# A hybrid token-mixer block: the scan's x tiles in two tiles of their own, requested two chunks ahead

## The chip, the cores and the metric

The kernel runs on one core of a Trainium2 chip. The metric is the device time of one execution in microseconds (us). Three executions of the kernel before took 1987.88, 1989.72 and 1990.76 us; their median, 1989.72 us, is the time that a change is held against. One further execution was profiled.

## What is computed

The reference is one layer of a streaming encoder over 1024 frames of width 1024, in float32. One input projection feeds three mixers that run side by side (latent attention, attention with forgetting, and a Mamba-2 scan), three sigmoid gates weigh them, and a gated feed-forward block with a short convolution follows. The change lies in the scan. Cut to it, the reference is:

```python
xBC = jax.nn.silu(causal_dwconv(xBC, conv_w, conv_b))
xs, Bm, Cm = jnp.split(xBC, [SSM_INNER, SSM_INNER + SSM_GROUPS * SSM_STATE], axis=-1)
...
xdt = xf * dtc[..., None]
cb = jnp.einsum('bcign,bcjgn->bcijg', Cc, Bc)
y_diag = jnp.einsum('bcijg,bcijgh,bcjghp->bcighp', cb, decay, xdt)
states = jnp.einsum('bcjgn,bcjgh,bcjghp->bcghpn', Bc, decay_to_end, xdt)
_, h_in = lax.scan(step, h0, (jnp.moveaxis(states, 1, 0), jnp.moveaxis(chunk_decay, 1, 0)))
y_off = jnp.einsum('bcign,bcghpn,bcigh->bcighp', Cc, h_in, jnp.exp(a_cum))
y = (y + xh * D[:, None]).reshape(Bsz, S, SSM_INNER)
return rms_norm(y * jax.nn.silu(z), norm_g)
```

The kernel scans in chunks of 128 frames, eight in all (`NT` = 8).

## The kernel before, in words

The work runs in stages, one behind the other on TensorE: projections, the convolution that makes x, B and C for the scan and stores them to `xbc_d` in DRAM (about 390 to 540 us of the profile), the two attentions (540 to 878 us), the scan (878 to about 1080 us), the branch projections, and the feed-forward block. Every matmul with two float32 operands is made of three products of high and low halves, so an operand is split first: ScalarE (ACT) writes the high half, VectorE (DVE) the low one.

The scan alone does not fill TensorE. So the attentions and the scan are interleaved with *fill*: the projections of the gates (`all_fill`, L1410 on, matmuls `mm` on L1428). A fill block loads a weight tile `wr` (L1392), splits it into `wh` and `wl` (L1399, L1400), makes two half-rows of a gate in PSUM, sends each through a tanh on ACT (L1406) into a row buffer `u`, and stores the row to `g_d` (L1438).

The row buffers are a ring of four tiles of 128x1024 float32 (`f_t4`, L1382, tag `t4`). Three kinds of tiles take turns in it: the fill's rows `u`, the scan's gate rows `zt` (L1968), and the scan's x tiles `xs` (L1906). All of them appear in the profile under the name `t`.

One chunk c of the scan goes through three steps.

- `ssd_a` (L1913): request B and C (`bc`) and the decay rows (`row`) of chunk c+1; transpose the eight 128x128 blocks of `xs` in two groups of four (`stp`, L1922), each copied by ACT into `xT` (L1923); request `xs` of chunk c+1 (L1927); transpose B and multiply C by B (L1933, L1935, into one `stp` tile), which DVE and ACT read on L1936 to L1938 (`bT` high and low, and `cbm`); then `xd` (DVE, L1941), `xdd` and `y` (GpSimd, L1945 and L1947), the split of `xdd` into `xddh` and `xddl`, and the decay matrices `E` (ACT L1954 and L1955, DVE L1956).
- `ssd_b` (L1966) one chunk later: request `zt`; the states (`pst`, L1964), the state `hst` (DVE L1979 to L1982), the products `py` (L1990), the part from the state before (`pof`) and the scaled output (L2008 to L2017, with a reciprocal root that goes back and forth between DVE and GpSimd).
- `ssd_c` (L2019) one more chunk later: transposes of the output (`stp`, L2025), copies to `yT` (L2026), and the store.

All `stp` tiles, whatever their step, take turns in two PSUM buffers (tag `tp`, two buffers): a transpose group waits until the readers of the group two before it are done.

What sets the order. TensorE runs in program order inside `manual_schedule`, and the program order comes from `merge` (L1470 on), which interleaves the three steps and the fill by a planned cost of each. The other engines and the DMA queue of the sync engine (SP) are ordered by the scheduler of the language, when the program is built; each then runs strictly in its order. Every load and store that matters here is issued on SP, so an issue that has to wait holds up all that stand behind it.

The pool `frp` (L1889) is opened ahead of the scan. In the kernel before its two tiles, `ws0` and `ws1` of 128x1024 float32, are first used after the scan, for two rows of attention output (`ar`, L2104) and then for sums of feed-forward weights (`ws_tiles`, L2069).

Of the kernel before, what the change touches and what calls it, by code (L numbers as in the profile page):

```python
# [11 lines left out]
F32 = mybir.dt.float32  # L12
# [9 lines left out]
P = 128  # L22
D = 1024
S = 1024
NT = S // P
# [17 lines left out]
def block_kernel(ctx: ExitStack, tc: tile.TileContext, x, positions, norm_mix_g, w_in, b_gate,  # L43
# [7 lines left out]
    def TP(name, bufs, **kw):  # L51
        if kw.get("space") != DRAM:
            kw["reuse_waits"] = "tile"
        return tc.tile_pool(name=name, bufs=bufs, **kw)
# [72 lines left out]
    def uid(s):  # L127
        cnt[0] += 1
        return f"{s}_{cnt[0]}"

    def split(h, l, src, he=None, le=None):
        he = he or A
        le = le or V
        i = A.activation(h, src, AF.Copy) if he is A else he.tensor_copy(h, src)  # L134
        return i, le.tensor_sub(l, src, f32(h))  # L135
# [489 lines left out]
    with ExitStack() as pm:  # L625
# [165 lines left out]
        def fx_bank():  # L791
            return acc("fx", "mv" if units % 3 == 2 else "mm")
# [243 lines left out]
    with ExitStack() as px:  # L1036
# [70 lines left out]
        for n, (which, c0) in enumerate(chunks):  # L1107
# [11 lines left out]
            for t in range(NT):  # L1119
# [8 lines left out]
                p = fx_head[t] if units < 6 else fx_bank()  # L1128
# [30 lines left out]
        for half in range(2):  # L1159
            p = fx_bank()  # L1160
# [30 lines left out]
    with ExitStack() as pc_:  # L1191
# [24 lines left out]
        def c_bank():  # L1216
            return psp.tile([P, 512], F32, name=uid("cb"), tag="up", bufs=6)
# [98 lines left out]
        for half in range(2):  # L1316
            p = c_bank()
# [64 lines left out]
    f_t4 = Ring(fpl, [P, S], F32, "t4", 4)  # L1382
# [67 lines left out]
    def advance(gen):  # L1450
        c = next(gen, None)
        while isinstance(c, list):
            for h in c:
                force(h)
            c = next(gen, None)
        if c is not None:
            clk[0] += c
            run_until(clk[0])
        return c
# [429 lines left out]
    frp = pfr.enter_context(TP("frp", 1, side="right"))  # L1889
    with ExitStack() as ps__:  # L1890
# [4 lines left out]
        def load_rows(o, c):  # L1895
            o.row = pool.tile([P, 16, P], F32, name=uid("row"), tag="row")
            for g in range(2):
                SY.dma_start(o.row[:, 8 * g:8 * g + 8, :],
                             cum_d[16 * c + 8 * g:16 * c + 8 * g + 8, :].partition_broadcast(P))

        def load_bc(o, c):
            o.bc = pool.tile([P, 4, P], F32, name=uid("bc"), tag="bc", bufs=3)
            SY.dma_start(o.bc, xbc_d[8:12, :, c * P:c * P + P].rearrange("j p s -> p j s"))

        def load_xs(o, c):
            o.xs, _ = f_t4.get()  # L1906
            o.xs = o.xs.rearrange("p (j s) -> p j s", j=8)
            SY.dma_start(o.xs, xbc_d[0:8, :, c * P:c * P + P].rearrange("j p s -> p j s"))

        def hb(t, c, hs=slice(0, 16)):  # L1910
            return t[:, c, hs].unsqueeze(2).to_broadcast([P, hs.stop - hs.start, 64])

        def ssd_a(o, c):  # L1913

            if c + 1 < NT:
                load_bc(obj[c + 1], c + 1)
                load_rows(obj[c + 1], c + 1)
            xT = pool.tile([P, D], F32, name=uid("xT"), tag="xT", bufs=1)
            for g in range(2):
                pt = psp.tile([P, 512], F32, name=uid("stp"), tag="tp", bufs=2)  # L1920
                for j in range(4):
                    T.transpose(pt[:, j * P:j * P + P], o.xs[:, 4 * g + j, :], ident)  # L1922
                A.activation(xT[:, 512 * g:512 * g + 512], pt, AF.Copy)  # L1923
                yield 0.44
            yield 0.0
            if c + 1 < NT:
                load_xs(obj[c + 1], c + 1)  # L1927
            o.bT = [pool.tile([P, 2, P], F32R, name=uid(n), tag=n) for n in ("bTh", "bTl")]
            o.c_ = [pool.tile([P, 2, P], F32R, name=uid(n), tag=n) for n in ("Ch", "Cl")]
            cbm = pool.tile([P, 2, P], F32, name=uid("cbm"), tag="cbm")  # L1930
            pt = psp.tile([P, 4, P], F32, name=uid("stp"), tag="tp", bufs=2)
            for g in range(2):
                T.transpose(pt[:, g, :], o.bc[:, g, :], ident)  # L1933
            for g in range(2):
                T.matmul(pt[:, 2 + g, :], o.bc[:, g, :], o.bc[:, 2 + g, :], start=True, stop=True)  # L1935
            split(*o.bT, pt[:, 0:2, :])  # L1936
            split(*o.c_, o.bc[:, 2:4, :])
            V.tensor_mul(cbm, pt[:, 2:4, :], tri.unsqueeze(1).to_broadcast([P, 2, P]))  # L1938
            xv = xT.rearrange("p (h d) -> p h d", d=64)
            o.xd = pool.tile([P, 16, 64], F32, name=uid("xd"), tag="xd")  # L1940
            V.tensor_mul(o.xd, xv, hb(dt, c))  # L1941
            o.xdd = [pool.tile([P, 16, 64], F32R, name=uid(n), tag=n, bufs=1) for n in ("xddh", "xddl")]
            xdd = pool.tile([P, 16, 64], F32, name=uid("xdd"), tag="xdd", bufs=1)
            if c + 1 < NT:
                G.tensor_mul(xdd, xv, hb(dend, c))  # L1945
            o.y = pool.tile([P, 16, 64], F32, name=uid("y"), tag="y", bufs=3)
            G.tensor_mul(o.y, xv, Db.unsqueeze(2).to_broadcast([P, 16, 64]))  # L1947
            yield 0.65
            o.E = []
            for q in range(4):  # L1950
                E = pool.tile([P, 4, P], F32, name=uid("E"), tag="E", bufs=4)
                for hh in range(4):
                    h = 4 * q + hh
                    A.activation(E[:, hh, :], o.row[:, h, :], AF.Relu, scale=-1.0, bias=cumc[:, c, h:h + 1])  # L1954
                A.activation(E, E, AF.Exp, scale=-1.0)  # L1955
                V.tensor_mul(E, E, cbm[:, q // 2:q // 2 + 1, :].to_broadcast([P, 4, P]))  # L1956
                o.E.append(E)
                if q == 1 and c + 1 < NT:
                    split(*o.xdd, xdd)
                yield 0.0  # L1960
# [71 lines left out]
        with tc.manual_schedule(engines={mybir.EngineType.PE}):  # L2032
            obj = {c: Head() for c in range(NT)}
            load_bc(obj[0], 0)
            load_xs(obj[0], 0)
            load_rows(obj[0], 0)
            merge([], 6.0)
            grain[0] = 4
            for c in range(NT + 2):
                st = []  # L2040
                if c < NT:
                    st.append((ssd_a(obj[c], c), 1.6))
                if 0 <= c - 2 < NT:
                    st.append((ssd_c(obj[c - 2], c - 2), *((0.88, 0.6) if c <= NT else (8.0, 0.2))))
                if 0 <= c - 1 < NT:
                    st.append((ssd_b(obj[c - 1], c - 1, obj.get(c - 2)), 6.4, 0.05))
                merge(st, FILL_SSD[c])
            for _ in range(4):
                if advance(fill) is None:
                    break  # L2050
# [234 lines left out]
    for t, nh in units:  # L2285
# [20 lines left out]
        p = head[t] if early else psp.tile([P, 512], F32, name=uid("wo"), tag="up", bufs=6)  # L2306
# [323 lines left out]
```

## Time and profile before

| | |
|---|---|
| median of three executions (lowest to highest) | 1989.72 us (1987.88 to 1990.76) |
| profiled execution, its own time | 1986.64 us |
| its span, first to last instruction | 1984.9 us |
| TensorE (PE) busy | 1958.7 us, 99% of the span |
| VectorE (DVE) / ScalarE (ACT) / GpSimd (POOL) busy | 70% / 49% / 35% |
| mean granted TensorE clock | 0.998 of full speed |

How to read the profile: all times are in us from the start of the span. A row of the timeline gives start, length, engine, line, operation, `output<-inputs` and, in brackets, how long the engine stood idle before the row and what ended that. `SPq` rows are issues of DMAs, not the transfers. A row of the chain of waits gives start and length of a piece of the chain that ended last. Matmuls overlap, so on PE the spacing of starts tells more than the length of one.

### The profile page before, as it was taken

What the parts mean: (1) busy time and instruction counts of PE and PEld (TensorE: products, weight loads), DVE (VectorE), ACT (ScalarE), POOL (GpSimd) and SP (SyncE); (2) the same over time, 40 slices, a digit from 0 to 9 for tenths busy, and PEclk for the clock granted to TensorE, in tenths of its full rate; (3) what the DMA queues carried; (4) which work ended last, traced back from release to release, by engine and by line L of the source; (5) the groups of instructions that cost most, each with busy time, mean ns of one, the idle gap of its engine ahead of it and who ended that gap; (6) DMA issues with size and microseconds to landing.
All of it is one profiled execution on the core that took longest, in us unless ns stands there. A gap on an engine that the chain in (4) does not pass through costs nothing.

```text
span 1984.9 us, 28475 instructions
## 1 busy us (share of the span) xinstructions
PE 1958.7 (99%) x10101; PEld 1668.1 (84%) x10101; DVE 1397.4 (70%) x2156; ACT 965.8 (49%) x1678; POOL 701.3 (35%) x666
## 2 busy tenths in 40 slices
PE   9999999999999999998999999999999999999999
PEld 8989888888899988887888888888878888888887
DVE  7777567879566766757884575558997777766555
ACT  5555322355466666766774232225554444544432
POOL 5133232056123222213340351101664444423655
PEclk9999999999999999999999999999999999999999
DMA  6166856333645556545665785333323211249575
GB/s 180 53 197 212 269 189 211 103 106 112 197 123 145 134 144 149 145 127 172 179 193 172 260 289 190 124 121 107 106 85 96 75 53 54 85 157 333 194 260 191
DMA packets 278409, 312.18 MB, mean 157 GB/s; under 512 B 19213, under 2 KB 209305, under 8 KB 278266
## 3 DMA queue, kind: packets, MB, share of 16 engines
q1 hardware_dynamic: 278264, 310.35, 50.5%
q8 instruction: 80, 1.31, 0.3%
q14 instruction: 63, 0.52, 0.1%
q10 hardware_dynamic: 2, 0.00, 0.0%
HBM read 217.17 MB, written 93.13 MB: 156 GB/s over the span
## 4 chain that ended last, share of the span: by engine, by line
PE 88%; DVE 4%; issue 3%; DMA 2%; ACT 2%; POOL 1%; SPq 0%; DVEq 0%; ACTq 0%; POOLq 0%
PE mm L1428 10%; PE dn L2577 10%; PE ybr L2145 9%; PE fx L798 7%; PE cb L1224 7%; PE ua L2236 6%; PE uc L2236 5%; PE ud L2236 5%; PE wo L2281 4%; PE s L1737 4%; PE tp L1804 3%; PE ub L2236 2%; PE fxv L188 2%; PE py L1990 1%; PE o L1824 1%
## 5 line engine op out<-in xcount | busy, mean ns | idle before, releaser
L1764 POOL TENSOR_SCALAR pm<-pm,rs 128x128 f32<-128x128 f32 (+7 forms) x128 | 95.2, 748 | 249.7 <-DVE rs L1762 217.3
L2577 PE MATMUL dn<-dr,dr 128*128 128x512 f32 x592 | 182.3, 389 | 0.0
L1428 PE MATMUL mm<-hnh,wh 128*128 128x512 f32 x320 | 133.1, 416 | 0.9 <-DVE o L1788 0.9
L2577 PEld LDWEIGHTS dn<-dr,dr 128*128 128x128 f32 x592 | 111.1, 188 | 22.9
L1428 PE MATMUL mm<-hnh,wl 128*128 128x512 f32 x320 | 126.4, 395 | 0.0
L1428 PE MATMUL mm<-hnl,wh 128*128 128x512 f32 x320 | 126.3, 395 | 0.0
L1756 ACT ACTIVATE pm<-s,nmx 128x128 f32<-128x128 f32 (+7 forms) x128 | 94.8, 741 | 64.6 <-DVE nmx L1751 56.3
L2577 PE MATMUL dn<-dr 128*128 128x512 f32 x296 | 115.3, 390 | 0.0
L1812 DVE TENSOR_TENSOR ptl<-tp,pth 128x512 fp32r<-128x512 f32 (+1 forms) x160 | 96.7, 631 | 24.5 <-ACT pth L1808 22.6
L135 DVE TENSOR_TENSOR dr<-dr,dr 128x1024 fp32r<-128x1024 f32 x52 | 73.0, 1413 | 51.2 <-ACT dr L134 41.8
L135 DVE TENSOR_TENSOR wl<-S,wh 128x1024 fp32r<-128x1024 f32 x55 | 82.9, 1507 | 34.8 <-ACT wh L134 34.8
L1751 DVE TENSOR_REDUCE nmx<-s 128x1 f32<-128x128 f32 (+7 forms) x128 | 93.5, 747 | 11.9 <-PE s L1737 7.4
L2145 PE MATMUL ybr<-al,wh 128*128 128x512 f32 x256 | 99.8, 390 | 0.0
L2145 PE MATMUL ybr<-ah,wl 128*128 128x512 f32 x256 | 99.8, 390 | 0.0
L2145 PE MATMUL ybr<-ah,wh 128*128 128x512 f32 x256 | 99.7, 389 | 0.0
L1808 ACT ACTIVATE pth<-tp 128x512 fp32r<-128x512 f32 (+1 forms) x160 | 82.6, 552 | 20.6 <-PE tp L1804 18.7
L134 ACT ACTIVATE wh<-wr 128x1024 fp32r<-128x1024 f32 (+1 forms) x47 | 42.4, 902 | 100.5 <-PE ybr L2145 39.5
L134 ACT ACTIVATE wh<-S 128x1024 fp32r<-128x1024 f32 x55 | 58.3, 1059 | 65.1 <-PE uc L2236 47.1
L134 ACT ACTIVATE dr<-dr 128x1024 fp32r<-128x1024 f32 x52 | 55.0, 1061 | 71.5 <-PE dn L2577 49.8
L1804 PE MATMUL tp<-ident,pm 128*128 128x128 f32 x576 | 81.1, 272 | 0.0
L135 DVE TENSOR_TENSOR wl<-wr,wh 128x1024 fp32r<-128x1024 f32 (+1 forms) x47 | 55.1, 1172 | 36.3 <-ACT wh L134 36.2
L2454 DVE SCALAR_TENSOR_TENSOR fa<-cg,pc_f,fa 128x1023 f32<-128x1023 f32 (+1 forms) x44 | 74.3, 1688 | 1.4 <-ACT fa L2449 1.4
(612 smaller groups left out, 6220.2 us busy)
## 6 DMA issues: line engine op xcount, KB each, us to landing
dr<-act_d SPq DMA_DIRECT2D x99, 256.0 KB
wr<-in_w_in_dram SPq DMA_DIRECT2D x35, 512.0 KB
gl<-g_d SPq DMA_DIRECT2D x24, 512.0 KB
wr<-in_ffn_w_up_dram SPq DMA_DIRECT2D x23, 512.0 KB
ws<-in_ffn_w_down_dram SPq DMA_DIRECT2D x22, 512.0 KB
wsum_d<-ws SPq DMA_DIRECT2D x22, 512.0 KB
act_d<-fa SPq DMA_DIRECT2D x22, 512.0 KB
g_d<-t SPq DMA_DIRECT2D x20, 512.0 KB
```

Source lines behind the costliest of these rows:

```text
L134: i = A.activation(h, src, AF.Copy) if he is A else he.tensor_copy(h, src)
L135: return i, le.tensor_sub(l, src, f32(h))
L798: T.matmul(p, a(k), b(k), start=k == 0 and i == 0, stop=k == NK - 1 and i == 2)
L1224: T.matmul(ps, a, b, start=first and i == 0, stop=i == 11, skip_group_check=not first)
L1428: T.matmul(ps, a[:, k, :], b[half][:, k, :], start=(k == 0 and i == 0), stop=(k == NK - 1 and i == 2))
L1756: A.activation(r.p[:, 0:cols], r.row, AF.Exp, bias=r.nmx[:, 0:1], accum_out=r.rs[:, 0:1])
L1764: r.norm = Task("G", (d - 0.025, d), lambda: G.tensor_scalar(r.p[:, 0:cols], r.p[:, 0:cols], r.rs[:, 1:2], 0.0, op0=ALU.mult, op1=ALU.add) ...
L1804: T.transpose(x.pt[:, c * P:c * P + P], rows_[qi].p[:, k * P:k * P + P], ident)
L1812: V.tensor_sub(x.tl[:, :off], x.pt[:, :off], f32(x.th[:, :off]))
L2145: T.matmul(pss[half], w_[:, k, :], a_[k][:, hs], start=k == 0 and i == 0, stop=k == nk - 1 and i == 2)
L2236: T.matmul(ps, a, b, start=first and n == 0, stop=n == 11, skip_group_check=not first)
L2577: T.matmul(ps[m], a[:, ts_], b[:, 512:], start=first_ and j == 0 and q == 0, stop=j == NFH - 1 and q == 2, skip_group_check=not first_)
```

## The change

The x tile of a chunk is no longer taken from the ring `f_t4`. It gets one of the two tiles `ws0` and `ws1` of the pool `frp`, the even chunks the first and the odd ones the second. The tiles of chunks 0 and 1 are requested ahead of the scan's loop, and chunk c requests the tile of c+2, instead of c+1, once its own transposes are in the program. The ring's four buffers are left to `u` and `zt`. Two tiles that live in `frp` after the scan (`ar`, L2104) now wait for the transposes of the last two x tiles.

```diff
         def load_xs(o, c):
-            o.xs, _ = f_t4.get()
-            o.xs = o.xs.rearrange("p (j s) -> p j s", j=8)
+            o.xs = frp.tile([P, 2, 512], F32, name=uid("xs"), tag=f"ws{c % 2}").rearrange(
+                "p a s -> p (a s)").rearrange("p (j s) -> p j s", j=8)
             SY.dma_start(o.xs, xbc_d[0:8, :, c * P:c * P + P].rearrange("j p s -> p j s"))
...
             yield 0.0
-            if c + 1 < NT:
-                load_xs(obj[c + 1], c + 1)
+            if c + 2 < NT:
+                load_xs(obj[c + 2], c + 2)
...
             load_bc(obj[0], 0)
-            load_xs(obj[0], 0)
+            for c in range(2):
+                load_xs(obj[c], c)
             load_rows(obj[0], 0)
```

The order of TensorE's and GpSimd's instructions is unchanged; only the name of the x tile differs in it. SP's queue changes at many places, DVE's and ACT's order at one place each (on ACT, the exponential of one `E` tile of chunk 2 and one tanh of the fill change places).

The first place is SP's queue at the end of the convolution stage and the beginning of the attentions. `xbc_d<-ca` is the last store of the convolution's output, `wr` a fill weight, `g_d` the gates' rows, `vv` and `qk` the values and the query and key tiles of the first attention heads. Before:

```order
L1238 DMA xbc_d<-ca_5757 128x1024
L1392 DMA wr_6379<-in_w_in_dram 128x8x128
L1309 DMA g_d_83<-cg_5692 128x1024
L1527 DMA vv_5892<-v_d 128x8x128
L1309 DMA g_d_83<-cv_5802 128x1024
L1522 DMA qk_1090_5894<-k_h 104x1024
```

In the same place now:

```order
L1238 DMA xbc_d<-ca_5757 128x1024
L1908 DMA xs_10582<-xbc_d 128x8x128
L1908 DMA xs_10584<-xbc_d 128x8x128
L1392 DMA wr_6379<-in_w_in_dram 128x8x128
L1309 DMA g_d_83<-cg_5692 128x1024
L1309 DMA g_d_83<-cv_5802 128x1024
L1527 DMA vv_5892<-v_d 128x8x128
L1522 DMA qk_1090_5894<-k_h 104x1024
```

The loads of the x tiles of chunks 0 and 1 stand right behind that store, ahead of both attentions, and the values of head 0 (`vv_5892`) stand behind one store more than before.

The second place is SP's queue at the beginning of the scan. `t<-xbc_d` is an x tile in the ring (the first row here is that of chunk 1, the second that of chunk 2), `t<-z_d` the `zt` of chunk 0, `g_d<-t` a fill row. Before:

```order
L1903 DMA bc_10753<-xbc_d 128x4x128
L1392 DMA wr_10821<-in_w_in_dram 128x8x128
L1898 DMA row_10755<-cum_d 128x1024 x2
L1438 DMA g_d_82<-t_2336_10591 128x1024
L1908 DMA t_2355_10697<-xbc_d 128x8x128
L1969 DMA t_2376_10778<-z_d 128x1024
L1908 DMA t_2394_10854<-xbc_d 128x8x128
L1903 DMA bc_10946<-xbc_d 128x4x128
```

In the same place now:

```order
L1903 DMA bc_10755<-xbc_d 128x4x128
L1392 DMA wr_10823<-in_w_in_dram 128x8x128
L1908 DMA xs_10699<-xbc_d 128x8x128
L1898 DMA row_10757<-cum_d 128x1024 x2
L1438 DMA g_d_82<-t_2337_10593 128x1024
L1969 DMA t_2377_10780<-z_d 128x1024
L1392 DMA wr_11018<-in_w_in_dram 128x8x128
L1903 DMA bc_10948<-xbc_d 128x4x128
```

The x tile of chunk 1 is gone from behind the fill row's store; the one x tile here is that of chunk 2 (`xs_10699`), and it now stands ahead of the decay rows.

The third place is DVE's order where chunk 1 of the scan is prepared and chunk 0 is finished. `xddl` is the low half of chunk 1's `xdd`, `y<-y,py` adds products to chunk 0's output, `y<-y,t` multiplies that output by `zt`. Before:

```order
L1941 TENSOR_TENSOR xd_10871<-xT_10758,dt 128x1024
L1400 TENSOR_TENSOR wl_10824<-wr_10821,wh_10823 128x1024
L135 TENSOR_TENSOR xddl_10874<-xdd_10875,xddh_10873 128x1024
L1993 TENSOR_TENSOR y_10720<-y_10720,py_10843 128x512
L2008 SCALAR_TENSOR_TENSOR y_10720<-y_10720,t_2376_10778 128x1024
```

In the same place now:

```order
L1941 TENSOR_TENSOR xd_10873<-xT_10760,dt 128x1024
L1400 TENSOR_TENSOR wl_10826<-wr_10823,wh_10825 128x1024
L1993 TENSOR_TENSOR y_10722<-y_10722,py_10845 128x512
L135 TENSOR_TENSOR xddl_10876<-xdd_10877,xddh_10875 128x1024
L2008 SCALAR_TENSOR_TENSOR y_10722<-y_10722,t_2377_10780 128x1024
```

The sum with `py`, which reads PSUM, and the low half of `xdd` have changed places.

## The prediction

> **What bounds the kernel now.** I read the page first, then the windows over the scan, the timeline of TensorE there, the chain of waits, and the timelines of the engines that TensorE waits for. The page says that TensorE is the bound:
>
> ```profile
> span 1984.9 us, 28475 instructions
> PE 1958.7 (99%) x10101; PEld 1668.1 (84%) x10101; DVE 1397.4 (70%) x2156; ACT 965.8 (49%) x1678; POOL 701.3 (35%) x666
> ```
>
> Only 1984.9 - 1958.7 = 26 us of the span are free of matmuls, so no change of a transfer's place can bring more than a piece of that, plus what a lowered clock costs beside it. The windows show where the piece is that this change touches (columns: stretch, its length, busy time of PE, PEld, DVE, ACT and POOL, granted clock, DMA share, GB/s):
>
> ```profile
> 885.00:905.00 20.00, 16.36 (x75) 13.36 (x74) 10.88 (x11) 12.51 (x31) 5.71 (x2) 0.92 0.96 314
> 925.00:945.00 20.00, 16.04 (x95) 14.04 (x94) 15.07 (x22) 14.56 (x32) 7.35 (x8) 0.94 0.34 113
> 945.00:965.00 20.00, 19.45 (x109) 16.60 (x107) 15.74 (x20) 13.35 (x30) 6.94 (x10) 0.97 0.61 182
> 965.00:985.00 20.00, 19.17 (x110) 16.67 (x111) 14.90 (x23) 14.39 (x31) 8.13 (x10) 1.00 0.66 197
> 985.00:1005.00 20.00, 19.99 (x118) 17.21 (x116) 16.99 (x26) 15.67 (x34) 8.27 (x10) 1.00 0.62 185
> ```
>
> TensorE is idle in the first chunks of the scan and not after 985. The idle stretches stand before three `stp` groups on L1922, the transposes of an x tile:
>
> ```profile
> 896.18 0.61 PE L1935 MATMUL stp<-bc 128*128 128x128 f32 x4
> 900.43 0.63 PE L1922 MATMUL stp<-ident,t 128*128 128x128 f32 x4 [3.64 <-DMA t<-xbc_d]
> 938.74 0.61 PE L2025 MATMUL stp<-ident,y 128*128 128x128 f32 x4
> 943.30 1.09 PE L1922 MATMUL stp<-ident,t 128*128 128x128 f32 x4 [3.96 <-issue]
> 965.83 0.63 PE L1922 MATMUL stp<-ident,t 128*128 128x128 f32 x4 [1.38 <-issue]
> ```
>
> Call them stall 1 (chunk 1), stall 2 (chunk 3) and stall 3 (chunk 4). Only stall 1 ends with the landing of an x tile. The chain of waits and SP's timeline show why that was late:
>
> ```profile
> 893.56 0.32 SPq L1438 DMA_DIRECT2D g_d<-t  x1
> 893.92 0.43 SPq L1908 DMA_DIRECT2D t<-xbc_d  x1
> ```
>
> ```profile
> 892.86 0.68 ACT t L1406
> 893.92 6.37 DMA t<-xbc_d
> 901.06 4.34 PE mm L1428 x12
> 906.79 2.75 PE mm L1428 x12
> 910.38 0.44 PE stp L1922 x4
> 944.39 3.59 PE mm L1428 x12
> ```
>
> The x load stood on SP behind the store of a fill row, which waited for a tanh that ended at 892.86 + 0.68 = 893.54; then it took 6.37 us while the DMA engines were 0.96 busy. The last rows show a second price: the twelve fill matmuls right behind stall 1 took 4.34 us against 2.75 for the same twelve later, 1.59 more, and the granted clock of that window is 0.92. Behind stall 2 they took 3.59.
>
> **What the change removes.** The x tile of chunk 1 is asked for ahead of both attentions, so stall 1 loses its cause: 3.64 + 1.59 = 5.23 us. That is the ceiling, not the sum, because other engines did not wait for that tile. The rows of DVE and ACT that TensorE needs next, and of POOL beside them:
>
> ```profile
> 898.46 2.80 DVE L135 TENSOR_TENSOR xddl<-xdd,xddh 128x1024 fp32r<-128x1024 f32 x1
> 901.19 0.41 DVE L135 TENSOR_TENSOR bTl<-stp,bTh 128x256 fp32r<-128x256 f32 x1
> 901.96 2.50 DVE L1956 TENSOR_TENSOR E<-E,cbm 128x512 f32<-128x512 f32 x4
> 906.13 1.39 DVE L1979 COPY hst<-pst 128x512 f32<-128x512 f32 x2 [1.67 <-PE pst L1964]
> 916.78 2.81 DVE L135 TENSOR_TENSOR xddl<-xdd,xddh 128x1024 fp32r<-128x1024 f32 x1
> 919.51 0.68 DVE L1993 TENSOR_TENSOR y<-y,py 128x512 f32<-128x512 f32 x1
> 920.22 1.23 DVE L2008 SCALAR_TENSOR_TENSOR y<-y,t 128x1024 f32<-128x1024 f32 x1
> 942.79 0.41 DVE L1938 TENSOR_TENSOR cbm<-stp,tri 128x256 f32<-128x256 f32 x1
> ```
>
> ```profile
> 907.55 1.06 ACT L134 ACTIVATE hsh<-hst 128x1024 fp32r<-128x1024 f32 x1 [5.81 <-DVE hst L1979]
> 909.36 1.06 ACT L1399 ACTIVATE wh<-wr 128x1024 fp32r<-128x1024 f32 x1 [0.74 <-PE mm L1428]
> 928.95 1.16 ACT L2017 ACTIVATE y<-y,yr 128x1024 f32<-128x1024 f32 x1 [5.25 <-POOL yr L180]
> ```
>
> ```profile
> 915.62 2.89 POOL L1947 TENSOR_TENSOR y<-xT,Db 128x1024 f32<-128x1024 f32 x1
> ```
>
> TensorE, step by step. Without stall 1 it goes on at 900.43 - 3.64 = 896.79, makes the four transposes (0.44) and twelve fill matmuls (2.75) and stands at 900.0 before the states `pst`, which in the old run began at 901.06 + 4.34 = 905.40. But `pst` needs `bTl`, and DVE has that at 901.19 + 0.41 = 901.60, unmoved: no row before it on DVE waits for the x tile of chunk 1. So a new stall of about 1.7 us stands there, and TensorE is 905.40 - 901.7 = 3.7 us early.
>
> DVE and ACT, step by step. DVE ends the products `E` at 901.96 + 2.50 = 904.46, unmoved. Then it waited 1.67 us for `pst`; that wait goes, and `hst` comes 1.67 earlier. ACT's `hsh` waits for `hst`, so it moves by 1.67. ACT's next step, `wh`, waited 0.74 for fill matmuls that now end before 906; that goes too. From there ACT is 1.67 + 0.74 = 2.4 us early, and with it what hangs on its copies of `xT`: POOL's `xdd`, then `xddl` on DVE.
>
> The swap on DVE adds a piece. `xddl` of 1024 elements took 2.81 us at 916.78, and ended 919.59 - 918.51 = 1.08 us after POOL's `y` (915.62 + 2.89), so it hardly ran while POOL did. A sum that reads PSUM (0.68) is now put in front of it, into that waiting time, and no longer behind it. DVE's L2008 comes 0.68 earlier still: 2.4 + 0.7 = 3.1 us. [...]
>
> From L2008 on the chain carries this 3.1 through: ACT's square of `y`, the root on POOL and DVE for which ACT waited 5.25 us, the rest of ACT's row, POOL's `xdd` of chunk 2, and DVE up to `cbm` of chunk 2 at 942.79. Stall 2 ends there, not with a transfer: `cbm` ends at 943.20, the transposes start at 943.30, and their PSUM buffer is the one that `cbm` reads. So TensorE arrives 3.7 us early at a stall whose end moves only by 3.1: stall 2 grows from 3.96 to about 4.6 us. Behind it the old order holds. ACT and DVE wait for TensorE there and move with it, stall 3 stays, and from 985 on there is no idle time that could take the gain back.
>
> **Other parts, costed at nothing.** The later x tiles wait on SP for the transposes of the chunk two before; SP stood there anyway. The tile of chunk 2 is now ahead of the decay rows, but it waits for the transposes of chunk 0, and the rows behind it wait for the last `E` of chunk 0, which comes later. `ar` in `ws1` waits for the transposes of the last chunk and is first read when the scan is over. If either cover were gone, the price is that of one load, 6.37 us at the most loaded place.
>
> **The early loads.** They add 1 MB to a stretch in which DMA is saturated, ahead of the values of head 0:
>
> ```profile
> 517.29 0.32 SPq L1238 DMA_DIRECT2D xbc_d<-ca  x1
> 531.69 0.32 SPq L1309 DMA_DIRECT2D g_d<-cv  x1
> ```
>
> ```profile
> 520.00:530.00 10.00, 10.00 (x46) 8.26 (x45) 3.13 (x4) 4.08 (x6) 2.57 (x2) 1.00 0.94 268
> 530.00:540.00 10.00, 10.00 (x46) 8.29 (x45) 0.43 (x1) 1.84 (x2) 0.00 (x0) 1.00 1.01 285
> ```
>
> ```profile
> vv<-v_d SPq DMA_DIRECT2D x2, 512.0 KB
> w0l<-q_h SPq DMA_DIRECT2D x1, 416.0 KB
> ```
>
> ```profile
> 548.73 0.29 PE L1816 MATMUL o<-pth,vv 128*128 128x256 f32 x1
> ```
>
> From 517.29 on, and up to these values, SP asks for two stores, four query and key tiles of at most 416 KB, two x tiles, a weight, two gate rows and the values: 8 x 0.524 + 4 x 0.426 = 5.9 MB. At 268 GB/s that is 22.0 us, so the values land at about 539.3, and not before 531.69, when the store ahead of them is issued. TensorE first reads them at 548.73. The cover is 9.4 us, so the term is nothing.
>
> **The sum.** 3.1 us less. The profiled execution took 1986.64, its span of 1984.9 and 1.7 around it, and would take 1986.64 - 3.1 = 1983.5. It lies 3.1 us below the median of 1989.72, inside the scatter; against the median the forecast is 1989.72 - 3.1 = 1986.6 us. A measurement of this kernel can tell about 0.2%, 4.0 us, from no change, so the forecast lies within what counts as the same.
>
> **The rivals.**
>
> Full gain. Stall 2 does not grow and the ceiling of 5.23 comes through, if `cbm` of chunk 2 moves as far as TensorE does. For it: ACT and DVE wait for TensorE at several rows. Against it: DVE's `E` ends at 904.46 whatever TensorE does. Time 1989.72 - 5.2 = 1984.5. Chance 0.17.
>
> A second slow stretch. Stall 1 and stall 2 were each followed by one stretch of lowered clock; a stall 2 of 4.6 us may be followed by more of it. Price: the 1.59 us seen once, again. Time 1989.72 - 3.1 + 1.6 = 1988.2. [...] Against it: part of a second slow stretch would lie under the stall itself. Chance 0.16.
>
> Slower: the values of head 0 come late. Place: the first `o` product of the attention, 548.73. It decides if the rate of the loads falls below 5.9 MB / (548.73 - 517.29) = 188 GB/s, and costs more than the gain below 5.9 / 34.5 = 171. At 140 GB/s they land at 559.4, 10.7 us late, and the time is 1989.72 - 3.1 + 10.7 = 1997.3. For it: the x loads are 512-byte pieces, 128 columns of 4 bytes. Against it: 268 and 285 GB/s in the rows above. Chance 0.07.
>
> That the change does not do what it says: SP's order shows that it does more, since the first two x tiles go far ahead of the two chunks. Had they stayed behind the fill row's store, nothing would move. The order leaves this no chance.
>
> **How the numbers follow.** The forecast has 0.60: 1986.6, with its own range from 1985.0 (the slow stretch behind stall 2 gone, 1.6 less) to 1988.1 (2.4 without the swap, and half a slow stretch, 0.8, more). Its lower fifth, 0.12, and the full gain, 0.17, are faster by over 0.2%, which begins at 1985.7: 0.29. The late values are slower: 0.07. The rest, 0.64, is within. The range reaches from the full gain less half a microsecond of scatter, 1984.0, past the second slow stretch with the scatter of the three runs above it, to 1989.8.
>
> **What would show it.** Right: no idle time at the `stp` group of chunk 1 around 896.8, about 1.7 us of it before `pst`, the twelve fill matmuls in between at 2.75; `hsh` at 905.9; DVE's L2008 3.1 earlier; stall 2 of about 4.6, ending at 940.1 with `cbm` just before; the same attention stage up to 878. Wrong: stall 2 of 3.96 or less (full gain), more slow matmuls behind it than the twelve of before (second slow stretch), or idle time before the first `o` product with a load named as its end (late values).

## The result, and the profile after

The changed kernel takes 1986.07 us (median of 22 runs, 1982.82 to 1989.55). The kernel before took 1989.76 beside it (22 runs, 1987.06 to 1993.16). The ratio is 0.9979 with a 95% interval of 0.9973 to 0.9986, which is 2.8 to 5.4 us. The profiled execution took 1986.45, with a span of 1984.7.

Two windows over the scan, in the columns of the prediction:

```profile
885.00:905.00 20.00, 19.02 (x92) 15.45 (x92) 10.84 (x12) 13.19 (x31) 5.72 (x2) 1.00 0.95 302
925.00:945.00 20.00, 15.57 (x80) 13.28 (x80) 15.58 (x19) 15.82 (x34) 6.09 (x5) 0.83 0.49 141
```

In the first window TensorE is busy for 19.02 us where it was for 16.36, and the clock is whole. In the second it is lower than before, 0.83 against 0.94. TensorE's timeline has the idle stretches:

```profile
897.33 0.60 PE L1922 MATMUL stp<-ident,xs 128*128 128x128 f32 x4
901.90 0.50 PE L1964 MATMUL pst<-xddl,bTh 128*128 128x512 f32 x1 [0.98 <-DVE xddl L135]
963.85 0.63 PE L1922 MATMUL stp<-ident,xs 128*128 128x128 f32 x4 [1.38 <-issue]
```

The transposes of chunk 1 wait for nothing now, a new wait of 0.98 us stands before the second `pst` product, and stall 3 is as it was. The chain of waits shows stall 2 and what runs behind it:

```profile
936.02 4.42 issue
940.44 1.09 PE stp L1922 x4
941.53 4.49 PE mm L1428 x12
```

Stall 2 grew from 3.96 to 4.42 us, and the twelve fill matmuls behind it take 4.49 instead of 3.59. DVE's and ACT's rows between the two stalls:

```profile
904.96 1.28 DVE L1979 COPY hst<-pst 128x512 f32<-128x512 f32 x2
914.52 0.68 DVE L1993 TENSOR_TENSOR y<-y,py 128x512 f32<-128x512 f32 x1
915.12 2.32 DVE L135 TENSOR_TENSOR xddl<-xdd,xddh 128x1024 fp32r<-128x1024 f32 x1
917.37 1.21 DVE L2008 SCALAR_TENSOR_TENSOR y<-y,t 128x1024 f32<-128x1024 f32 x1
939.93 0.41 DVE L1938 TENSOR_TENSOR cbm<-stp,tri 128x256 f32<-128x256 f32 x1
```

```profile
907.23 1.04 ACT L1399 ACTIVATE wh<-wr 128x1024 fp32r<-128x1024 f32 x1
```

`hst` and `wh` have lost their waits. To compare the times, one thing has to be taken out: this execution came to the scan 0.70 us later than the one of before, and 0.66 of that is there already at the store on L1238 (517.29 before, 517.95 now), ahead of the first early load (522.25). The first transposes of the scan and the first product of the branch stage, in before and then in the changed kernel:

```profile
885.49 0.60 PE L1922 MATMUL stp<-ident,t 128*128 128x128 f32 x4
1079.15 0.39 PE L2145 MATMUL ybr<-ah,wh 128*128 128x512 f32 x1
```

```profile
886.19 0.60 PE L1922 MATMUL stp<-ident,xs 128*128 128x128 f32 x4
1077.15 0.39 PE L2146 MATMUL ybr<-ah,wh 128*128 128x512 f32 x1
```

From the one to the other is called the scan's length here: 193.66 us before, 190.96 now, 2.70 less. What comes behind it took 905.75 us before (span 1984.9 less 1079.15) and 907.55 now. The part that is later now shows in the branch stage, as waits that the profile of before didn't have:

```profile
1132.95 0.50 PE L2146 MATMUL ybr<-ah,wh 128*128 128x512 f32 x1 [0.37 <-ACT wh L134]
1134.81 0.50 PE L2146 MATMUL ybr<-ah,wl 128*128 128x512 f32 x1 [1.13 <-DVE wl L135]
```

So two questions are left: is stall 1 the whole gain, and are the branch stage's waits part of the change?

### The profile page after: what moved, and what is told of

Its sections match the earlier page's. It is cut to its first block, busy times and chain, and to the rows that moved or that the text cites. A ratio compares the mean times of both kernels' runs of the same rounds, so it can differ in the third digit from the quotient of the medians.

```text
span 1984.7 us, 28482 instructions
## 1 busy us (share of the span) xinstructions
PE 1958.4 (99%) x10101; PEld 1666.5 (84%) x10101; DVE 1395.4 (70%) x2156; ACT 965.3 (49%) x1678; POOL 705.3 (36%) x666
## 4 chain that ended last, share of the span: by engine, by line
PE 86%; DVE 4%; DMA 3%; issue 3%; ACT 2%; POOL 1%; SPq 1%; DVEq 0%; ACTq 0%; POOLq 0%
PE dn L2578 10%; PE mm L1428 10%; PE ybr L2146 7%; PE fx L798 7%; PE cb L1224 7%; PE ua L2237 6%; PE uc L2237 5%; PE ud L2237 5%; PE wo L2282 4%; PE s L1737 4%; PE tp L1804 3%; PE ub L2237 2%; PE fxv L188 2%; PE py L1990 1%; PE o L1824 1%
## 5 line engine op out<-in xcount | busy, mean ns | idle before, releaser
L135 DVE TENSOR_TENSOR wl<-wr,wh 128x1024 fp32r<-128x1024 f32 (+1 forms) x47 | 54.0, 1149 | 34.8 <-ACT wh L134 34.7
```

## The experiments

The two theories that are told apart first: **A**, the gain is stall 1 alone, and it came from one load's place on SP. **C**, the free ring and the second chunk of lead bring part of it. Scan length and idle time of TensorE by stall, from one profile of each kernel (before_again and after_again are second profiles of the two kernels), and the ratio of its times to the kernel before, all in us but the ratio:

| kernel | scan | before `stp` 1 | before `pst` | stall 2 | stall 3 | branch stage | behind the scan | ratio, 95% |
|---|---|---|---|---|---|---|---|---|
| before | 193.66 | 3.64 | 0 | 3.96 | 1.38 | 0 | 905.75 | 1 |
| before_again | 193.85 | 3.87 | 0 | 3.98 | 1.38 | 1.68 | 908.25 | |
| changed | 190.96 | 0 | 0.98 | 4.43 | 1.38 | 1.69 | 907.55 | 0.9979 (0.9973 to 0.9986) |
| after_again | 190.46 | 0 | 1.15 | 4.43 | 1.38 | 1.13 | 907.87 | |
| chunk1_only | 191.21 | 0 | 0.97 | 4.43 | 1.38 | 0.79 | 906.47 | 0.9982 (0.9973 to 0.9991) |
| held_to_scan | 189.96 | 0 | 1.47 | 3.53 | 1.38 | 0.98 | 906.29 | 0.9977 (0.9968 to 0.9986) |
| all_but_chunk1 | 197.60 | 6.37 | 0 | 3.99 | 1.38 | 1.82 | 908.14 | 1.0017 (1.0008 to 1.0025) |
| swap_only | 193.99 | 3.55 | 0 | 3.25 | 1.38 | 2.12 | 909.76 | 0.9998 (0.9990 to 1.0007) |
| early_loads_fivefold | 191.19 | 0 | 1.35 | 4.43 | 1.38 | 0.91 | 907.46 | |
| fill_moved | 190.23 | 0 | 1.29 | 1.69 | 2.50 | 1.66 | 908.85 | 0.9966 (0.9952 to 0.9979) |
| fill_moved_more | 194.92 | 0 | 1.04 | 0 | 5.92 | 1.75 | 907.69 | 1.0004 (0.9995 to 1.0012) |
| cbm_first | 189.48 | 0 | 1.19 | 3.36 | 1.38 | 0.98 | 907.77 | 0.9969 (0.9957 to 0.9980) |
| held_and_cbm_first | 189.20 | 0 | 1.54 | 2.84 | 1.38 | 1.80 | 909.27 | 0.9968 (0.9956 to 0.9979) |
| fill_moved_cbm_first | 187.63 | 0 | 1.19 | 0.56 | 2.29 | 1.09 | 907.72 | 0.9960 (0.9947 to 0.9973) |

The scan's length is the first `ybr` less the first `stp` of the scan, "behind the scan" is the span less the first `ybr`. In fill_moved_more and fill_moved_cbm_first the stall 3 column is all idle time of 950 to 970, also ahead of the transposes of `y`.

### chunk1_only: one tile early, the rest as before

```diff
-            o.xs, _ = f_t4.get()
-            o.xs = o.xs.rearrange("p (j s) -> p j s", j=8)
+            if c == 1:
+                o.xs = frp.tile([P, 2, 512], F32, name=uid("xs"), tag="ws1").rearrange(
...
-            if c + 1 < NT:
+            if 2 <= c + 1 < NT:
...
-            load_xs(obj[0], 0)
+            for c in range(2):
+                load_xs(obj[c], c)
```

Expected: 

> The kernel before with one edit: the x tile of chunk 1 alone has its own tile and is asked for ahead of everything; all other x tiles stay in the ring, one chunk ahead. Theory A (stall 1 is the whole gain): the same time as the full change, 0.2% below before, ratio 0.9975 to 0.9985; no idle at the stp of chunk 1, stall 2 of 4.3 to 4.7 us. Rival C (freeing the ring and the second chunk of lead bring part of it): ratio 0.999 or more, or stall 2 above 5 us or stall 3 above 1.8.

Measured: ratio 0.9982 (0.9973 to 0.9991), no idle time at the transposes of chunk 1, stall 2 of 4.43. The scan's length is 191.21, 0.25 us more than in the first profile of the changed kernel, which had the same 6.82 us of lowered clock behind stall 2. So the seven other tiles add nothing that these runs can show, as theory A has it.

### all_but_chunk1: the full change, with one load left where it was

```diff
+            if c == 0:
+                load_xs(obj[1], 1); behind_(obj[1].xsl, stores[-1])
             if c + 2 < NT:
                 load_xs(obj[c + 2], c + 2)
...
-            for c in range(2):
-                load_xs(obj[c], c)
+            load_xs(obj[0], 0)
```

`stores` holds the stores of the fill rows, `xsl` is a chunk's x load, and `behind_` puts one instruction behind another in its queue's order.

Expected: 

> The full change (two tiles of their own, two chunks ahead, the first tile ahead of the attentions), except that the load of chunk 1's x tile stays where it was before on SP, right behind the store of the fill row; DVE's order of y and xddl in chunk 0 is then the old one. Theory A (stall 1 is the whole gain and comes from that place on SP): stall 1 of 3 to 4 us ended by the DMA of the tile, a slow stretch behind it, stall 2 near 3.96; ratio to before 0.9993 to 1.0003. Rival C (the free ring and the lead of the later chunks bring part of it): ratio 0.9988 or less, or stalls 2 and 3 shorter than 3.8 and 1.2.

Measured: ratio 1.0017 (1.0008 to 1.0025), slower than before, which neither theory had. SP's timeline and the chain of waits of this kernel:

```profile
892.32 0.36 SPq L1908 DMA_DIRECT2D xs<-xbc_d  x1
893.21 1.28 SPq L1898 DMA_DIRECT2D row<-cum_d  x2
895.14 0.32 SPq L1438 DMA_DIRECT2D g_d<-t  x1
895.51 0.73 SPq L1908 DMA_DIRECT2D xs<-xbc_d  x1
```

```profile
895.51 9.18 DMA xs<-xbc_d
904.83 1.08 PE stp L1922 x4
```

The first load is chunk 2's, which goes ahead of the rows and the fill row's store now that its tile is free; the last is chunk 1's. That one took 6.37 us before and 9.18 here, and stall 1 is 6.37 instead of 3.64. The clock is lowered for 6.83 us at stall 1 and again at stall 2, where it was 3.41 each time in the kernel before. Two chunks of lead without chunk 1's early place cost 3.9 us of scan. The tile's own buffer was free here, so its place on SP is enough to make the stall. In chunk1_only the early place alone removed it. C falls, with its sign the wrong way round.

### held_to_scan: the lead taken away, the place kept

```diff
+            behind_(obj[1].xsl, obj[0].bcl)
             load_rows(obj[0], 0)
```

`bcl` is chunk 0's load of B and C.

Expected: 

> The full change, but the x tile of chunk 1 is asked for only at the scan's start, right behind the first tile of B and C and ahead of the decay rows, not ahead of the attentions. Theory A (what made it late was its place on SP behind a store that waits for tanh, not the short lead): issued at about 880, landed in 3 to 7 us, ten us before the transposes of chunk 1 at 896.6; ratio 0.9972 to 0.9985, the same as the full change. Rival D (the lead itself counts, since DMA is 0.96 busy at the scan's start and the load pushes the decay rows and bc tiles back): the load is late by more than 1 us, or the E rows of chunk 0 come 1 us or more later; ratio 0.999 or more.

Measured: ratio 0.9977 (0.9968 to 0.9986). SP asks for the tile at 882.23:

```profile
882.23 0.50 SPq L1908 DMA_DIRECT2D xs<-xbc_d  x1
882.77 1.05 SPq L1898 DMA_DIRECT2D row<-cum_d  x2
```

TensorE waits for nothing at the transposes of chunk 1 at 898.73. In the changed kernel it was asked for at 522.25, so 360 us of lead are not needed; a place ahead of the rows is enough. Rival D is right in one point: the load does push the decay rows back. ACT's first `E` row of chunk 0, in the changed kernel and then here:

```profile
886.37 3.93 ACT L1954 ACTIVATE E<-row,strict 128x128 f32<-128x128 f32 x13 [0.66 <-DMA row<-cum_d]
888.75 1.59 ACT L1954 ACTIVATE E<-row,strict 128x128 f32<-128x128 f32 x5 [1.67 <-DMA row<-cum_d]
```

Counted from the scan's first transposes (886.19 and 887.55) it comes 1.02 us later, and the wait before `pst` is 1.47 instead of 0.98, but the time shows no loss. Stall 2 is 0.9 shorter here. Half of that is TensorE's later arrival (0.45 us). The other half is an earlier end (0.44 us): DVE's order moved once more, and L2008 of chunk 0, now ahead of `xddl`, ends 0.6 us earlier.

```profile
916.41 0.68 DVE L1993 TENSOR_TENSOR y<-y,py 128x512 f32<-128x512 f32 x1
917.12 2.21 DVE L2008 SCALAR_TENSOR_TENSOR y<-y,t 128x1024 f32<-128x1024 f32 x1
```

### swap_only: DVE's order alone

```diff
-                    split(*o.xdd, xdd)
+                    xl = split(*o.xdd, xdd)[1]
+                    if c == 1:
+                        behind_(xl, obj[0].ya)
```

`ya` is the sum `y` on L1993.

Expected: 

> The kernel before, with only DVE's order changed: the sum y on L1993 (last half of chunk 0) is put ahead of xddl of chunk 1, as in the changed kernel; the x tile stays late. Theory A (the sum goes into the time in which xddl waits for POOL): L2008 comes 0.7 us earlier relative to the first stp of the scan than in before (34.7 us behind it there), cbm of chunk 2 0.7 earlier, stall 1 stays at about 3.6, and stall 2 shrinks from 3.96 to about 3.3; time 0.7 less, ratio 0.9990 to 1.0000. [...]

Measured: ratio 0.9998 (0.9990 to 1.0007), which cannot tell 0.7 us from nothing. The row expected 34.0 us behind the scan's first transposes (34.7 less 0.7) stood at 919.99 - 885.15 = 34.84, so that expectation is missed. The cause is in front of it: at stall 1 the clock was lowered for 6.83 us in this execution and for 3.41 in before's, and TensorE came to stall 2 0.8 later. From the step that both have ahead of the swap, `wl`, to L2008 the rows are, in before and then here:

```profile
913.81 2.93 DVE L1400 TENSOR_TENSOR wl<-wr,wh 128x1024 fp32r<-128x1024 f32 x1
920.22 1.23 DVE L2008 SCALAR_TENSOR_TENSOR y<-y,t 128x1024 f32<-128x1024 f32 x1
```

```profile
914.29 2.92 DVE L1400 TENSOR_TENSOR wl<-wr,wh 128x1024 fp32r<-128x1024 f32 x1
917.74 2.33 DVE L135 TENSOR_TENSOR xddl<-xdd,xddh 128x1024 fp32r<-128x1024 f32 x1
919.99 1.22 DVE L2010 SCALAR_TENSOR_TENSOR y<-y,t 128x1024 f32<-128x1024 f32 x1
```

That is 6.41 and 5.70 us: 0.71 less, and `xddl` took 2.33 instead of 2.81. Stall 2 shows the same: this chain and TensorE both came 0.8 later, and the stall is 3.25 instead of 3.96, 0.71 less, as expected. The swap brings the 0.7 that the prediction gave it; an order that only exchanged two lengths would have brought nothing.

### The second profiles of both kernels

Expected of after_again: 

> The changed kernel once more, for a second profile. Theory A (the gain is stall 1, and the branch stage's waits of the first profile are part of the change): no idle time at the stp group of chunk 1, 0.5 to 1.5 us before the second pst, stall 2 of 4.3 to 4.7 us, and in the branch stage the ybr groups on L2146 again wait 1 us or more on wl, 1.7 us in all, because the chain of att_d loads did not move with TensorE. Rival B (that loss is scatter of one execution): stalls as in A, but under 0.5 us idle in the branch stage. [...]

Expected of before_again: 

> The kernel before once more, for a second profile. Stalls 1, 2 and 3 as in the first: 3.4 to 3.8, 3.96 and 1.38 us. Theory B (the branch stage's waits are scatter, a load of an attention row that takes 3.5 or 5 us, in both kernels): its time is 1 to 2 us of idle time there longer than the first profile's (which had none) when the time is near the median of 1989.7. Rival: none there again, and the time near the median comes from elsewhere.

Measured: 1986.93 and 1989.66 us. The same waits in the branch stage, in the kernel before:

```profile
1135.63 0.50 PE L2145 MATMUL ybr<-ah,wh 128*128 128x512 f32 x1 [0.33 <-ACT wh L134]
1137.48 0.50 PE L2145 MATMUL ybr<-ah,wl 128*128 128x512 f32 x1 [1.13 <-DVE wl L135]
```

after_again has 1.13 us of waits there, between what its two theories gave. Two things vary. The waits end a chain that begins with an attention row, asked for when DVE's `mg` has freed a tile of the ring. That row took 5.11 us here, 5.01 in the first profile of the changed kernel and 3.59 in its second. The wait on `wl` has another cause: that subtraction on DVE and a sum on POOL, `ws`, start within 0.02 us of each other, and one of the two takes 1.83 us. The first profile of before, then that of the changed kernel:

```profile
1133.53 0.69 DVE L135 TENSOR_TENSOR wl<-wr,wh 128x512 fp32r<-128x512 f32 x1 [0.65 <-ACT wh L134]
1133.54 1.83 POOL L942 TENSOR_TENSOR ws<-ws,ws 128x512 f32<-128x512 f32 x1
```

```profile
1132.93 1.83 DVE L135 TENSOR_TENSOR wl<-wr,wh 128x512 fp32r<-128x512 f32 x1 [0.65 <-ACT wh L134]
1132.94 1.27 POOL L942 TENSOR_TENSOR ws<-ws,ws 128x512 f32<-128x512 f32 x1
```

In both second profiles it was `wl` as well (1.82 and 1.83). So theory B of before_again holds in that both kernels have these waits, but the row's length alone does not make them. What is new in the changed kernel's profile is that the first profile of before lacked them. That one, with 905.75 us behind the scan against 906.3 to 909.8 in all others, was a short execution. Stall 1 of before_again, 3.87, lies just above the 3.4 to 3.8 that were expected.

The slow matmuls behind stall 2 differ between the two profiles of the changed kernel, 4.49 and 3.75 us for the twelve, with 6.82 and 3.42 us of lowered clock at the same stall of 4.43. The second, beside the 941.53 row above:

```profile
942.43 3.75 PE mm L1428 x12
```

### early_loads_fivefold: the attention's values pushed back

```diff
             for c in range(2):
-                load_xs(obj[c], c)
+                for _ in range(5):
+                    load_xs(obj[c], c)
```

Expected: 

> The changed kernel, with each of the two early x loads issued five times into the same tile, so that about three more of them stand ahead of the values of head 0 on SP, each waiting for the landing of the one before. Theory A (the values have some 9 us of cover): the values are issued 8 to 14 us later than in the changed kernel (532.78), land at 546 to 556 and TensorE waits 0 to 6 us ahead of the first o product or of the scores; the time rises by no more than that. Rival G (late values): if the two plain loads had already used most of the cover, TensorE waits 10 us or more, and the time is 10 us or more above the changed kernel's.

Measured: 1984.80 us in one execution, and no idle time of TensorE from 500 to 560. The values' load:

```profile
535.18 1.56 SPq L1527 DMA_DIRECT2D vv<-v_d  x1
```

Three more x loads went ahead of it, but it is asked for only 2.4 us later than in the changed kernel (532.78), or 4.0 from the store on L1238 (516.31 here, 517.95 there), against 8 to 14 expected. So this run presses less than meant. What it shows: 3 x 0.524 = 1.6 MB more ahead of the values costs nothing.

### fill_moved and fill_moved_more: work put ahead of stall 2

```diff
+    FILL_SSD[2] += 2.6
+    FILL_SSD[3] -= 2.6
```

and, for the second, `FILL_SSD[2] += 4.4` with 2.2 less for entries 3 and 8. `FILL_SSD` has the fill planned for each step of the scan's loop, in us; entry 8 is the step behind the last chunk.

Expected of fill_moved: 

> The changed kernel with twelve fill matmuls (2.75 us) of chunk 3's share given to chunk 2, so that they stand ahead of stall 2 and no longer behind pst of chunk 2. Theory A (stall 2 is set by DVE's cbm of chunk 2, which TensorE's fill does not feed): stall 2 falls from 4.43 to 1.6 to 1.9 us and the twelve matmuls behind it cost 2.75 to 3.6; time 2 to 4 us below the changed kernel, ratio to before 0.9955 to 0.9970. Rival F (the sums y, E and the state wait for TensorE's steps, so what is put ahead delays cbm as much, or stall 3 grows by what chunk 3 lost): stall 2 above 3, or stall 3 above 3; ratio 0.9975 to 0.9985.

Expected of fill_moved_more: 

> The changed kernel with twenty-four fill matmuls (5.5 us) ahead of stall 2: twelve from chunk 3's share, twelve from that of chunk 8. Theory A: stall 2 gone (0 to 0.3 us), no slow matmuls behind it, and time 4 to 6 us below the changed kernel, ratio to before 0.9945 to 0.9962, if the chunk that gives them up has no stall of its own. Rival F: ACT's tanh and DVE's splits of the fill rows come in between and move cbm later by over 2 us, or a stall of 2 us or more opens in chunk 3 or ahead of the branch stage; ratio 0.997 or more.

Measured: fill_moved has stall 2 at 1.69 us, as expected, and stall 3 at 2.50 instead of 1.38, with a clock lowered for 6.83 us from 958.21 on, in the midst of that stall. Of the 2.74 us that stall 2 lost, 1.1 came back at stall 3; the ratio is 0.9966 (0.9952 to 0.9979). fill_moved_more has no stall 2, but its ratio is 1.0004 (0.9995 to 1.0012), and rival F was right:

```profile
958.78 1.11 PE L2028 MATMUL stp<-ident,y 128*128 128x128 f32 x4 [5.92 <-ACT y L2020]
```

The next stall waits for ACT's scaled output `y`, and that came 4.5 us later than in the changed kernel (957.58 - 886.59 against 952.67 - 886.19). POOL's rows show why:

```profile
951.73 1.90 POOL L1948 TENSOR_TENSOR xdd<-xT,dend 128x1024 f32<-128x1024 f32 x1
953.91 1.90 POOL L1950 TENSOR_TENSOR y<-xT,Db 128x1024 f32<-128x1024 f32 x1
955.80 1.75 POOL L180 TENSOR_SCALAR yr<-rg_t,yr 128x1 f32<-128x1 f32 x1
```

The products `xdd` and `y` of the next chunk stand between the steps of the reciprocal root `yr`, and a step of 0.26 us takes 1.75; in the changed kernel the root was done before `xdd`. So fill ahead of a stall covers it, but the next one grows. In fill_moved chunk 3 has less fill of its own, which fits the 1.1 us but was not tried alone; in fill_moved_more the order on POOL moved too.

### cbm_first and its two combinations

```diff
-                    split(*o.xdd, xdd)
+                    xs_ = split(*o.xdd, xdd)
+                    if c in (2,):
+                        behind_(xs_[0], bTh)
+                        behind_(xs_[1], cb)
```

`bTh` is the high half of the transposed B, `cb` the product `cbm`. fill_moved_cbm_first has this for chunks 2 and 3 and the table of fill_moved; held_and_cbm_first has the load order of held_to_scan.

Expected of cbm_first: 

> The changed kernel with one order changed in chunk 2: bTh on ACT and bTl and cbm on DVE stand ahead of the split of xdd (xddh 1.06 us, xddl 2.27) and no longer behind it. Theory A (stall 2 ends when DVE has freed the PSUM buffer with bTl and cbm, and these only stand in a queue): cbm about 2.2 us earlier, stall 2 of 2.0 to 2.4 us instead of 4.43, at most one slow stretch of the clock behind it, pst of chunk 2 no later than that; time 2 to 4 us below the changed kernel, ratio to before 0.9957 to 0.9970. Rival H (something else feeds stall 2, or xddl, now late, holds pst of chunk 2 instead): stall 2 above 4, or 1.5 us or more of idle time before pst of chunk 2; ratio 0.9972 to 0.9985.

Expected of held_and_cbm_first: 

> The order of cbm_first together with the x tile of chunk 1 asked for at the scan's start (held_to_scan), where L2008 of chunk 0 stands ahead of xddl of chunk 1 on DVE. Theory A (both act on the chain to cbm of chunk 2 and add up): stall 2 of 0.9 to 1.6 us, no slow stretch behind it, ratio to before 0.9950 to 0.9965. Rival: the one makes the other idle, ratio as the better of the two alone.

Expected of fill_moved_cbm_first: 

> The changed kernel with twelve fill matmuls moved from chunk 3 to chunk 2 (fill_moved) and the order of cbm_first in chunks 2 and 3. Theory A (stalls 2 and 3 both wait for a cbm that stands behind xddl): stall 2 of 0 to 0.3 us (1.69 less 2.2), stall 3 of 0.3 to 0.8 (2.56 less 2.2), no slow stretch; 4 to 6 us below the changed kernel, ratio to before 0.9945 to 0.9960. Rival H: the late xddl opens stalls before pst of chunks 2 and 3 of together 2 us or more; ratio 0.9962 or more.

Measured: cbm_first has stall 2 at 3.36 us, 1.07 less, where 2.0 to 2.4 us of stall were expected; its ratio is 0.9969 (0.9957 to 0.9980), inside the expected range although the stall is not; its profile has 3.42 us of lowered clock at stall 2 and not 6.82. DVE's rows of the changed kernel and then of this one say why:

```profile
933.60 2.27 DVE L135 TENSOR_TENSOR xddl<-xdd,xddh 128x1024 fp32r<-128x1024 f32 x1 [0.58 <-ACT xddh L134]
935.79 0.41 DVE L135 TENSOR_TENSOR Cl<-bc,Ch 128x256 fp32r<-128x256 f32 x1
```

```profile
932.83 2.12 DVE L135 TENSOR_TENSOR Cl<-bc,Ch 128x256 fp32r<-128x256 f32 x1
938.68 0.41 DVE L1938 TENSOR_TENSOR cbm<-stp,tri 128x256 f32<-128x256 f32 x1
939.01 1.21 DVE L135 TENSOR_TENSOR xddl<-xdd,xddh 128x1024 fp32r<-128x1024 f32 x1
```

Without `xddl` in that place the next subtraction, `Cl`, takes 2.12 us instead of 0.41, and `xddl` takes 1.21 later on. The long time moved to another instruction that starts beside POOL's work: POOL's `y` runs from 932.44 to 934.79 in the changed kernel, and POOL is busy up to 934.67 here. `cbm` came 0.91 us earlier, counted from the scan's first transposes, and TensorE 0.15 later, which together make the shorter stall. held_and_cbm_first is no better in time, as its rival had it (0.9968, stall 2 of 2.84 where 0.9 to 1.6 was expected). fill_moved_cbm_first misses its stalls (0.56 and 2.29 us, expected up to 0.3 and 0.8) and has 3.41 us of lowered clock where none was expected. It has the shortest scan all the same, 187.63 us, and a ratio of 0.9960 (0.9947 to 0.9973): its median is 1983.73 us against 1986.07 for the change alone, and the two intervals only touch.

## Why the prediction was right, and where its terms were off

The time came out as forecast, 1986.07 against 1986.6, and the mechanism did: stall 1 goes, a new wait before `pst` takes back part of what TensorE gains, and stall 2 grows because its end moves less than TensorE's arrival. That the size fits so well is in part luck: the end of stall 2 moved by more than forecast, and a lowered clock behind it took some of that back in most profiles. By the prediction's own steps, with the 0.70 us of later start taken out:

- **Stall 1 and the clock behind it.** Gone, and the clock of that window is 1.00. TensorE stood at 897.33 - 0.70 = 896.63 before the transposes of chunk 1; forecast 896.79.
- **The wait before `pst`.** Forecast 1.7 us, 0.98 measured (0.97 to 1.54 in the other kernels with this load early). The step named `bTl` as what `pst` needs. The row names `xddl`: the first product runs at once, the second needs `xddl`, and `bTl` is first needed by the third. So TensorE was 4.0 us early at stall 2 (939.34 - 936.02 + 0.70) and not 3.7.
- **DVE and ACT.** L2008 came 920.22 - 917.37 + 0.70 = 3.55 us earlier; forecast 3.1. Of that, 0.7 is the swap, as swap_only shows. No row of the prediction had that sum beside a product of POOL, so its 0.7 was an estimate; in the changed kernel the sum took 0.68 at 914.52, with POOL's `y` running from 913.49 to 916.37. The other 2.83 are ACT's two waits (909.36 - 907.23 + 0.70 for `wh`); forecast 2.4. `cbm` of chunk 2 moved by 942.79 - 939.93 + 0.70 = 3.56, the same, so the chain carried it through whole.
- **Stall 2.** Forecast about 4.6, 4.43 measured in both profiles. With it fell the rival of the full gain, which had a stall 2 of 3.96 or less.
- **Behind stall 2.** Here the sum was short of a term in the first profile: the fill matmuls took 0.90 more, since the clock was lowered for 6.82 us and not for 3.41. The scan's gain fell from 3.56 to 2.7 by that. In the second profile the twelve took 0.16 more and not 0.90, and the scan is 3.2 to 3.4 shorter than in the two of before. The prediction held this as a rival of its own, with the price 1.6 and a chance of 0.16. Of the four profiles with a stall 2 of 4.43, three have 6.82 us of lowered clock (the first of the changed kernel, chunk1_only, early_loads_fivefold), at 0.7 to 1.2 us for the twelve: the price was too high and the chance too low. Part of the slow stretch lies under the stall, as the prediction had it (from 938.32, in a stall from 936.02 to 940.44). Every slow stretch in the scan, in all these profiles, lasted 3.41 to 3.42 or 6.82 to 6.83 us, read from windows of half a microsecond.
- **Early loads.** The attention stage is unchanged (336.8 us from its first `o` product to the scan's first transposes, in both kernels), and three more such loads brought no idle time there either, so the late values have no part in it.
- **Not foreseen: the branch stage.** It costs the changed kernel 1.1 to 1.7 us in its two profiles, and the kernel before 0 and 1.7. The prediction took the first profile's 1986.64 for a typical execution less scatter; it was one without these waits. Both kernels have them, but two profiles of each cannot show whether they weigh the same in the two medians.

The measured 2.8 to 5.4 us hold the forecast 3.1; the profiled scans, 2.7 to 3.4 us shorter, lie in their lower part or just below it. Whether a part beyond the scan is gained, these profiles can't say: what lies behind the scan varies by 4.0 us from one execution to another (905.75 to 909.76).

## What to carry to other kernels

When a load lands late, look first at what stands ahead of it on the queue that issues it: here a store that waited for a tanh, so a place ahead of the rows was worth as much as 360 us of lead (a ratio of 0.9977 against 0.9979). Freeing a buffer moves loads too: the one that no longer waits can push in front of the one that is late, and cost as much as the stall did (3.9 us of scan in all_but_chunk1, for a stall of 3.64 before). And carry an early engine through to the next point where it waits for the others; the gain is how far the end of that wait moves, not how long the stall was.

## What the runs showed of the hardware

In the scans of both kernels, DVE's subtractions `wl` and `xddl` of 128x1024, both inputs in SBUF, took 2.13 to 2.93 us where they started 1.0 us or more before the end of one of POOL's products `xdd` and `y`, and 1.21 to 1.23 elsewhere. Which one took long went with the place in DVE's order: in the changed kernel `xddl` came first, with 2.27, and `Cl` behind it took 0.41; in cbm_first `Cl` came first, with 2.12, and `xddl` later took 1.21. The sum that reads PSUM took 0.68 beside POOL's `y` (at 914.52 in the changed kernel), and 0.68 with POOL idle (at 919.51 in the kernel before). Steps on POOL differed as well: `ws` on L942 took 1.83 in the first profile of before and 1.27 in that of the changed kernel, and a `yr` step 1.75 in fill_moved_more and 0.26 in the changed kernel (at 951.13). Of `ws` and `wl`, in the two profiles of each kernel, the long time fell on `ws` once (1.83) and on `wl` three times (1.82 to 1.83).

A lowered clock went with a short idle stretch too: in fill_moved one of 2.50 us, from 956.86 to 959.36, with 6.83 us at half clock. In the four profiles with two slow stretches, their starts lie 40.96 us apart (before, 901.72 and 942.68; before_again, 902.20 and 943.16) or 44.37 (all_but_chunk1, 901.66 and 946.03; swap_only, 898.57 and 942.94), which is 12 and 13 times 3.413. The two slow pieces of fill_moved, and the one ahead of them (same columns as the windows above):

```profile
954.79:958.21 3.42, 2.06 (x19) 1.82 (x18) 3.42 (x5) 3.42 (x10) 0.00 (x0) 1.00 0.27 108
958.21:961.62 3.41, 2.27 (x8) 2.01 (x9) 3.41 (x7) 2.84 (x7) 0.00 (x0) 0.50 0.55 128
961.62:965.04 3.42, 3.42 (x10) 2.65 (x9) 2.53 (x5) 1.15 (x2) 0.77 (x2) 0.50 1.02 282
```

The piece with 2.06 us of matmuls was followed by a slow one, and that, with 2.27, by another. Around stall 3 of the kernel before, a piece with 2.03 us, which begins six steps of 3.413 behind the start of its second slow stretch, was not:

```profile
963.16:966.57 3.41, 2.03 (x18) 1.78 (x18) 3.41 (x7) 3.41 (x11) 0.00 (x0) 1.00 0.16 35
966.57:969.99 3.42, 3.42 (x17) 2.81 (x16) 3.42 (x6) 2.19 (x5) 0.05 (x1) 1.00 1.07 251
```

So in these rows the busy time of a piece does not tell alone whether a slow one follows; what decides it is not shown here.
